# A two-layer hybrid block on one core: pooling groups moved to the front, the last expert's order changed, and expert outputs written by index into one zeroed table

## The chip, the core and the metric

The kernel runs on one core of a Trainium2 chip. The metric is the device time of one execution in microseconds; three executions gave a median of 1464.87 us. The engines are TensorE (PE in the profile; PEld is its weight load), VectorE (DVE), ScalarE (ACT), GpSimd (POOL) and SyncE (SP), which here only issues DMAs. The clock that a profile shows for TensorE is the granted one, as a share of its full speed: 1.00 is 2.4 GHz and 0.50 is 1.2 GHz.

## The reference

Two layers work on 256 tokens of width 1024 and, in layer 0, on 256 context tokens as well (512 tokens in layer 0, 256 in layer 1). A layer is a token mixer of four branches (a Fourier mix, a pooling mix, global attention, window attention), each gated by the normalized input, and a mixture of 16 experts in four groups of four. Cut to what matters here:

```
h   = modulate(rms_norm(x, norm1), sh1, sc1)
# branches: a Fourier, b global attention, c window attention, d pooling
pool: for window w of (2, 4, 8, 16), one per group g of 128 columns:
        pooled[g] = moving_mean(p_in[g], w) - p_in[g]
      out_d[g] = (pooled[g] @ pool_w[g]) * pool_scale[g]
merged = sum_i sigmoid(h @ w_gate[i] + b_gate[i]) * (branch_i @ w_branch[i])
x  = x + g1 * (merged @ w_out)
h2  = modulate(rms_norm(x, norm2), sh2, sc2)
# two experts of one group per token, weights w_top
moe(h2) = sum_e combine[:, e] * ((silu(h2 @ w1[e]) * (h2 @ w3[e])) @ w2[e])
x  = x + g2 * moe(h2)
```

The output is a final RMSNorm of x. All arithmetic is float32.

## The kernel before

Every float32 product is made of three float16 matmuls: each operand is split into a high and a low half, and `mm3` (L577 to L582) adds hi x hi, hi x lo and lo x hi in PSUM. The weights come as float32 by SyncE's DMAs (L219) into tiles called stage, ext or X; ScalarE writes the high half (`whi`, L319), VectorE the low half (`wlo`, L323), and TensorE uses both. So each chunk of weights passes SyncE's queue, ScalarE and VectorE before TensorE has it. All DMAs of SyncE go through one queue in program order. The order within an engine is the order in which a scheduler laid out the program; instructions marked with `keep_in_program_order` stay where the code has them.

**The token mixer.** Global attention runs first, then window attention, each over units of one head pair and one block of queries. A unit's scores S are matmuls of L792 to L796; VectorE takes the row maxima (mx, nm), ScalarE the exponentials E (L811), and both write P in two halves (L824, L825). SyncE transposes P by DMA (into `pair` in layer 0 and `pt` in layer 1), and `values` (L840, output po) multiplies it with V. Between the steps of two units the code calls `next(fill)`: fill is a generator that hands out pieces of other work so that TensorE has something to do while the softmax runs. In window attention it is

```
fill = with_side(chain(spread(gated(1), pool_front(), SPREAD[l]), pool_back(), gated(3)), EV[l][1])
```

`gated(i)` makes branch i's gates (matmuls of hH and hL with a w_gate chunk, a tanh on ScalarE called gate) and multiplies them with the branch matmuls (w_branch). `pool_group(g)` makes the input of pooling group g on TensorE, copies it to SBUF (pool and poolp, L941 and L942), forms the moving sum by shifted additions on VectorE (L944, L947; L955 ends them), and splits the result into pmH and pmL. `mix(g)` multiplies these with the pooling matrix (pwH, pwL) and writes a quarter of branch d (ScalarE L975, VectorE L976). `spread` interleaves the steps of its two generators. Before the change `pool_front` makes groups 0 to 2, and `pool_back` does mix 0, group 3 interleaved with mixes 1 and 2, and mix 3. pmH and pmL have three buffers.

**The experts.** The router gives each token a slot in its two experts; an expert has 96 slots (CAP). `dispatch` gathers a group's tokens by matmuls with one-hot matrices. `up` makes the two hidden products (w1, w3), `hidden` joins them (sa: ScalarE L1388, VectorE L1389; hd is its split), and `down(e)` multiplies by w2 in two halves of 512 columns (py). For experts 0 to 13 ScalarE copies each half to a tile ys (L1333) and issues its DMA into the DRAM tensor `ydram`, 96 rows of 2 KB (L1334). Experts 14 and 15 stay on the chip as yHL and are added by matmuls. `index` computes for each token the two rows of ydram it needs (idx; rows of late experts become row 0 with weight 0). `fetch` (a copy `late` of idx on VectorE, L1445) issues the gathers on GpSimd's queue (L1405: one indirect DMA of 128 rows of 4 KB for each choice and block of 128 tokens), and `combine` weights and adds them (ScalarE L1412, VectorE L1413; in layer 1 also L1415 and L1416, which multiply by the gate g2 and add to x). Each layer has a ydram of its own. In layer 1, `fetch` runs in expert 14's step; in expert 15's step `combine(0)` stands after `up(15, "w1")` and `combine(1)` after `down(14)`. After the 16 experts a branch leads to further rounds for experts with more than 96 tokens; it is not taken with these inputs.

## Time and profile before

| What | Value |
|---|---|
| median of 3 executions | 1464.87 us (1464.43 to 1466.42) |
| the profiled execution's own time | 1468.68 us |
| its span in the trace | 1466.9 us |
| mean granted clock of TensorE | 0.978 |
| TensorE / VectorE / ScalarE / GpSimd busy | 1352.5 / 1119.0 / 953.2 / 14.0 us |
| DMA packets and bytes | 146416, 383.31 MB |
| window attention of layer 0, by the trace | about 240 to 374 us |
| experts of layer 0 | about 575 to 860 us |
| window attention of layer 1 | about 1000 to 1085 us |
| experts of layer 1 | about 1184 to 1445 us |

The trace is one execution; its times count from the span's start. A busy time is the sum of an engine's instructions in a stretch. A wait names the engine and line that waited and what ended the wait. A group of instructions is all those of one line, engine and operation. Matmuls are pipelined, so the length of one is longer than the step from one to the next. For a DMA, the time to landing counts from its issue. A tile's or line's row gives durations as minimum / median / maximum in ns.

### The profile page before, as it was taken

How to read it: one execution, taken by the hardware profiler on the slowest of the kernel's cores; microseconds unless marked ns; L12 is line 12 of the kernel's file. 1: busy time of each engine (PE TensorE's matmuls, PEld its weight loads, DVE VectorE, ACT ScalarE, POOL GpSimd, SP SyncE). 2: the span in 40 equal slices, each digit the busy share in tenths (PEclk: the TensorE clock that was granted, in tenths of full speed). 3: DMA queues.
4: the chain of work that ended last, by engine and by line, in shares of the span. 5: the costliest groups of instructions: out<-in, count | busy, mean ns of one | idle time of the engine just before them, and what ended most of it. 6: DMA issues, size and time to landing. Idle time of an engine off the chain costs nothing. (4 is left out here: it accounts for less than half of the span.)

```text
span 1466.9 us, 33640 instructions
## 1 busy us (share of the span) xinstructions
PE 1352.5 (92%) x14151; PEld 927.0 (63%) x14151; DVE 1119.0 (76%) x2003; ACT 953.2 (65%) x1431; POOL 14.0 (1%) x16
## 2 busy tenths in 40 slices
PE   5999999998999998999999978899989989999984
PEld 3545454444444585777777747587768767777762
DVE  3887647877354557888988888868957888989986
ACT  3777535655233337889898655856845579899971
POOL 0000000000000000000000110000000000000010
PEclk9999999999899999999999999999999999999997
DMA  9559762797685337799999564774979779999981
GB/s 365 207 131 226 228 207 87 198 232 202 187 340 191 120 111 259 270 337 419 397 420 380 222 248 177 188 234 116 232 240 361 263 280 341 418 419 419 399 327 52
DMA packets 146416, 383.31 MB, mean 261 GB/s; under 512 B 91856, under 2 KB 93904, under 8 KB 108112
## 3 DMA queue, kind: packets, MB, share of 16 engines
q1 hardware_dynamic: 133136, 355.24, 68.8%
q10 hardware_dynamic: 11392, 19.56, 3.6%
q0 software_dynamic: 1728, 6.29, 1.2%
q8 instruction: 112, 1.84, 0.5%
q14 instruction: 48, 0.39, 0.1%
HBM read 344.88 MB, written 15.20 MB: 245 GB/s over the span
## 5 line engine op out<-in xcount | busy, mean ns | idle before, releaser
L580 PE MATMUL mm<-hH,whi 128*128 128x96 f16 (+2 forms) x1824 | 398.5, 261 | 3.3 <-ACT whi L319 2.6
L582 PE MATMUL mm<-hH,wlo 128*128 128x96 f16 (+2 forms) x1824 | 398.1, 261 | 1.0 <-DVE wlo L323 0.9
L323 DVE SCALAR_TENSOR_TENSOR wlo<-stage,whi 128x1024 f16<-128x1024 f32 (+1 forms) x212 | 318.9, 1522 | 105.0 <-ACT whi L319 104.3
L581 PE MATMUL mm<-hL,whi 128*128 128x96 f16 (+2 forms) x1824 | 398.2, 261 | 0.0
L580 PEld LDWEIGHTS <-whi 128*128 128x128 f16 x3104 | 304.9, 98 | 75.2 <-issue 4.4
L319 ACT ACTIVATE whi<-stage 128x1024 f16<-128x1024 f32 (+1 forms) x212 | 269.8, 1294 | 126.2 <-PE mm L581 87.1
L582 PEld LDWEIGHTS <-wlo 128*128 128x128 f16 x3104 | 305.0, 98 | 73.7 <-DVE wlo L323 2.7
L581 PEld LDWEIGHTS <-whi 128*128 128x128 f16 x3104 | 305.0, 98 | 72.2 <-issue 2.1
L323 DVE SCALAR_TENSOR_TENSOR wlo<-ext,whi 128x2048 f16<-128x2048 f32 x116 | 262.1, 2287 | 43.2 <-ACT whi L319 43.2
L319 ACT ACTIVATE whi<-ext 128x2048 f16<-128x2048 f32 x116 | 217.8, 1904 | 9.9 <-PE mm L582 7.4
L582 PE MATMUL mm<-xg,wlo 128*128 128x96 f16 x1024 | 132.3, 206 | 0.0
L580 PE MATMUL mm<-xg,whi 128*128 128x96 f16 x1024 | 132.3, 206 | 0.0
L581 PE MATMUL mm<-xg,whi 128*128 128x96 f16 x1024 | 132.3, 206 | 0.0
L581 PE MATMUL py<-wlo,hd 128*96 128x512 f16 x240 | 90.9, 379 | 8.9 <-DVE wlo L323 8.7
L582 PE MATMUL py<-whi,hd 128*96 128x512 f16 x240 | 90.2, 381 | 6.8 <-DVE hd L321 6.0
L580 PE MATMUL py<-whi,hd 128*96 128x512 f16 x240 | 91.0, 379 | 0.0
L580 PE MATMUL mm<-brH,whi 128*128 128x512 f16 (+1 forms) x256 | 83.5, 326 | 0.0
L582 PE MATMUL mm<-brH,wlo 128*128 128x512 f16 (+1 forms) x256 | 83.4, 326 | 0.0
L581 PE MATMUL mm<-brL,whi 128*128 128x512 f16 (+1 forms) x256 | 83.4, 326 | 0.0
L1270 PE MATMUL mm<-Dg,merged 128*128 128x384 f16 x384 | 70.3, 336 | 3.8 <-DVE Dg L1203 1.8
L500 PE MATMUL mm<-stage,cpad 128*32 128x256 f32 x768 | 58.5, 408 | 13.7 <-DMA stage<-in_w_ada_dram 13.6
L825 DVE SCALAR_TENSOR_TENSOR P<-E,rl,P 128x512 f16<-128x512 f32 (+1 forms) x96 | 59.2, 659 | 8.4 <-ACT P L824 8.2
(313 smaller groups left out, 2054.2 us busy)
## 6 DMA issues: line engine op xcount, KB each, us to landing
ext<-in_w_dram SPq DMA_DIRECT2D x118, 1024.0 KB, 9.3
stage<-in_w_dram SPq DMA_DIRECT2D x62, 1024.0 KB, 9.1
stage<-in_w_ada_dram SPq DMA_DIRECT2D x48, 1024.0 KB, 6.0
stage<-in_w_gate_dram SPq DMA_DIRECT2D x32, 1024.0 KB, 5.8
stage<-in_w_in_dram SPq DMA_DIRECT2D x16, 1024.0 KB, 6.7
stage<-in_w_branch_dram SPq DMA_DIRECT2D x32, 512.0 KB, 4.1
ydram<-ys ACTq DMA_DIRECT2D x56, 192.0 KB, 6.9
stage<-in_w_out_dram SPq DMA_DIRECT2D x8, 1024.0 KB, 6.1
```

The lines of the kernel that those rows point to most:

```text
L319: a = nc.scalar.activation(hi, src, AF.Copy, scale=scale)
L323: b = nc.vector.scalar_tensor_tensor(lo, src, scale, hi, op0=ALU.mult, op1=ALU.subtract)
L500: pe.matmul(ps[32 * j:32 * j + 32, :], self.cpad[:, 2 * k:2 * k + 32], st[:, k, :], start=k < 4, stop=k >= 4, tile_position=(0, 32 * j))
L580: pe.matmul(ps, wH(k), xH(k), start=first and k == 0, stop=False)
L581: pe.matmul(ps, wH(k), xL(k), start=False, stop=False)
L582: pe.matmul(ps, wL(k), xH(k), start=False, stop=last and k == nk - 1)
L825: dve.scalar_tensor_tensor(pv[:, 1, qt, :], E[qt][:, 0:nk], r[:, qt:qt + 1], pv[:, 0, qt, :], op0=ALU.mult, op1=ALU.subtract)
L1270: pe.matmul(ps[:, 0:SLOTS], h2[n][t][:, cs(k)], Dg[:, t].rearrange("p e c -> p (e c)"), start=t == 0, stop=t == ntt - 1)
```

## The change

It has five parts.

- **Pooling.** `pool_front` makes all four groups, so group 3 is interleaved with gated(1) as well; `pool_back` is the four mixes alone. pmH and pmL have four buffers.
- **One table, zeroed.** ydram is made once, for both layers. `clear_rows` writes zeros to a seventh of it: a memset of a 128x512 tile on VectorE and one DMA of SyncE (3 x 128 rows of 2 KB, 786 KB). It is called in each unit of layer 0's window attention until the table is done, seven times.
- **Indirect writes.** The two halves of an early expert's output go to ydram by an indirect DMA on GpSimd's queue instead of ScalarE's DMA. Each of the 96 slots has a row number in `rows`; those of empty slots lie outside the table, and the DMA skips them.
- **`filled`.** Six small VectorE operations per layer make `rows` from the counts of the experts, after expert 0's `hidden`. The counts become a lasting tile, and a column of constants is added.
- **End of layer 1.** `combine(0)` moves from behind `up(15, "w1")` to behind `down(14)`, and `combine(1)` from there to behind `hidden(15)`.

```
-LASTING = ("posm", "cw", "cb", "nri", "sp", "se", "ch16")
+LASTING = ("posm", "cw", "cb", "nri", "sp", "se", "ch16", "cnt")
...
+        self.ydram = self.dram.tile([(NE - LATE) * CAP, D], F32, "ydram")
+        self.unset = list(range(0, 21, 3))
...
+    def clear_rows(self):
+        if self.unset:
+            a = self.unset.pop()
+            z = self.wk.tile([128, 512], F32, "zero", tag="t2")
+            self.nc.vector.memset(z, 0.0)
+            rows = self.ydram.rearrange("s (h c) -> (s h) c", h=2).rearrange("(a p) c -> p a c", p=128)
+            self.nc.sync.dma_start(rows[:, a:a + 3, :], z.unsqueeze(1).to_broadcast([128, 3, 512]))
...
-                  {"pmH": 3, "pmL": 3, "a2": 3, "P": 3, "pt": 2 - full, "E": 3, "G": 2})
+                  {"pmH": 4, "pmL": 4, "a2": 3, "P": 3, "pt": 2 - full, "E": 3, "G": 2})
...
+                if full and not glob:
+                    self.clear_rows()
                 next(fill, None)
...
         def pool_front():
             pool_weights()
-            for g in range(3):
+            for g in range(4):
                 yield from pool_group(g)
...
-            mix(0)
-            yield
-            last = pool_group(3)
-            for g in range(1, 3):
-                next(last, None)
+            for g in range(4):
                 mix(g)
                 yield
-            yield from last
-            mix(3)
             pooled["done"] = True
...
-        ydram = self.dram.tile([early * CAP, D], F32, "ydram")
+        ydram = self.ydram
...
-                        act.dma_start(ydram[e * CAP:(e + 1) * CAP, hs], ys)
+                        if not self.dry:
+                            yh = ydram.rearrange("s (h c) -> (s h) c", h=2)
+                            gp.indirect_dma_start(out=yh, in_=ys, in_offset=None,
+                                                  out_offset=bass.IndirectOffsetOnAxis(ap=rows[0:CAP, half, e:e + 1], axis=0),
+                                                  bounds_check=2 * early * CAP - 1, oob_is_err=False)
...
+            def filled():
+                rf = sm.tile([128, 16], F32, "rowf")
+                TT(rf, C("part").to_broadcast([128, 16]), cnt, op=ALU.is_ge)
+                dve.tensor_tensor(rf[0:1, 0:1], rf[0:1, 0:1], rf[0:1, 0:1], op=ALU.subtract)
+                dve.scalar_tensor_tensor(rf, rf, BIG, C("part").to_broadcast([128, 16]), op0=ALU.mult, op1=ALU.add)
+                dve.scalar_tensor_tensor(rf, C("slot", 0, 16), float(CAP), rf, op0=ALU.mult, op1=ALU.add)
+                for half in range(2):
+                    dve.tensor_scalar(rows[:, half, :], rf, 2.0, float(half), op0=ALU.mult, op1=ALU.add)
...
                 pa = up(e, "w1")
-                if e == NE - 1 and pe_all:
-                    combine(0, True)
...
                     down(e - 1, prev)
                 if e == NE - 1 and pe_all:
-                    combine(1, True)
+                    combine(0, True)
...
                 prev = hidden(e, pa, pb)
+                if e == NE - 1 and pe_all:
+                    combine(1, True)
+                if e == 0:
+                    filled()
```

How this moves instructions shows at three places. In the rows, `x2` is two such instructions in a row, and the line numbers of the changed kernel are its own (L319 becomes L320, L323 L324, L811 L823, L824 L836, L1013 L1021, L975 L989, L1413 L1425).

ScalarE at the end of layer 0's window attention, before; L824 is P, L811 E, L319 with po the split of the attention output, L941, L942 and pmH a pooling group, L975 a mix:

```order
L941 ACTIVATE pool_4356<-mm 128x256
L942 ACTIVATE poolp<-mm 128x256
L811 ACTIVATE E,ls<-S,nm 128x256 x2
L816 ACTIVATE es<-nm,sink 128x2
L824 ACTIVATE P<-E,rl 128x256 x2
L319 ACTIVATE brH_2938<-po 128x256
L811 ACTIVATE E,ls<-S,nm 128x256 x2
L816 ACTIVATE es<-nm,sink 128x2
L444 DMA sink<-in_sink_dram 128x8
L319 ACTIVATE pmH<-poolp 128x256
L824 ACTIVATE P<-E,rl 128x256 x2
L975 ACTIVATE brH_4189<-mm,psl 128x512
```

And in the changed kernel, the last units of the same attention:

```order
L320 ACTIVATE whi<-stage 128x1024
L836 ACTIVATE P<-E,rl 128x256 x2
L823 ACTIVATE E,ls<-S,nm 128x256 x2
L828 ACTIVATE es<-nm,sink 128x2
L320 ACTIVATE whi<-stage 128x1024
L836 ACTIVATE P<-E,rl 128x256 x2
L1021 ACTIVATE gate<-mm,hbg 128x512
L320 ACTIVATE adah<-mm 128x256
L823 ACTIVATE E,ls<-S,nm 128x256 x2
L828 ACTIVATE es<-nm,sink 128x2
L456 DMA sink<-in_sink_dram 128x8
L836 ACTIVATE P<-E,rl 128x256 x2
```

The pooling copies and both pmH are gone from among the last units; the last mix now stands ahead of these rows, and a gate and weight splits stand between the units.

ScalarE at the end of layer 1's window attention, before; gate is the tanh of gated(3):

```order
L319 ACTIVATE whi<-stage 128x1024
L975 ACTIVATE brH_19113<-mm,psl 128x256
L824 ACTIVATE P<-E,rl 128x512 x2
L319 ACTIVATE whi<-stage 128x1024
L941 ACTIVATE pool_19154<-mm 128x256
L942 ACTIVATE poolp<-mm 128x256
L975 ACTIVATE brH_19113<-mm,psl 128x256 x2
L319 ACTIVATE whi<-stage 128x1024
L319 ACTIVATE brH_18273<-po 128x256
L319 ACTIVATE pmH<-poolp 128x256
L975 ACTIVATE brH_19113<-mm,psl 128x256
L1013 ACTIVATE gate<-mm,hbg 128x256
```

And in the changed kernel:

```order
L989 ACTIVATE brH_19313<-mm,psl 128x256 x3
L320 ACTIVATE whi<-stage 128x1024
L836 ACTIVATE P<-E,rl 128x512 x2
L320 ACTIVATE brH_18424<-po 128x256
L989 ACTIVATE brH_19313<-mm,psl 128x256
L320 ACTIVATE whi<-stage 128x1024
L1021 ACTIVATE gate<-mm,hbg 128x256
L320 ACTIVATE whi<-stage 128x1024
L1021 ACTIVATE gate<-mm,hbg 128x256
L320 ACTIVATE brH_18424<-po 128x256
```

The last split of po now comes after two gates, where it came before the last mix and the first gate; no pooling copy is left.

VectorE in the last expert of layer 1, before; L1296 and L1297 are slot weights, yHL with py the output split of expert 14, wlo from X the last weight split, L1413, L1415 and L1416 the combination:

```order
L1445 COPY late<-idx 128x4
L1296 TENSOR_SCALAR slotw_25133<-mm 96x2
L1297 TENSOR_TENSOR slotw<-slotw_25133 96x1
L323 SCALAR_TENSOR_TENSOR wlo<-ext,whi 128x2048 x2
L1413 SCALAR_TENSOR_TENSOR yg<-yg,wr 128x1024
L323 SCALAR_TENSOR_TENSOR yHL<-py,slotw,yHL 96x512
L1415 TENSOR_TENSOR yg<-yg,merged 128x1024
L323 SCALAR_TENSOR_TENSOR wlo<-X_24636,whi 128x2048
L1416 TENSOR_TENSOR X_4729<-X_4729,yg 128x1024
L323 SCALAR_TENSOR_TENSOR yHL<-py,slotw,yHL 96x512
L1413 SCALAR_TENSOR_TENSOR yg<-yg,wr 128x1024
L1389 SCALAR_TENSOR_TENSOR sa<-mm,sa 128x384
```

And in the changed kernel, where these three lines are L1425, L1427 and L1428:

```order
L1457 COPY late<-idx 128x4
L1304 TENSOR_SCALAR slotw_25344<-mm 96x2
L324 SCALAR_TENSOR_TENSOR wlo<-ext,whi 128x2048
L1305 TENSOR_TENSOR slotw<-slotw_25344 96x1
L324 SCALAR_TENSOR_TENSOR wlo<-X_24847,whi 128x2048
L324 SCALAR_TENSOR_TENSOR yHL<-py,slotw,yHL 96x512 x2
L1425 SCALAR_TENSOR_TENSOR yg<-yg,wr 128x1024
L1427 TENSOR_TENSOR yg<-yg,merged 128x1024
L1425 SCALAR_TENSOR_TENSOR yg<-yg,wr 128x1024
L1428 TENSOR_TENSOR X_4751<-X_4751,yg 128x1024
L1401 SCALAR_TENSOR_TENSOR sa<-mm,sa 128x384
```

The last weight split and both output splits moved ahead of the first step of the combination; sa of expert 15 stands behind four steps of the combination, as before, but all four now come right ahead of it.

On GpSimd's queue, 28 writes a layer now stand ahead of the gathers, and each waits for the landing of the one before it. On SyncE's queue the seven DMAs of zeros stand among the loads and transposes of layer 0's window attention.

## Rows read from the trace of the kernel before

**Rows 1.** The page: busy time, share of the span and instructions of each engine.

```profile
PE 1352.5 (92%) x14151; PEld 927.0 (63%) x14151; DVE 1119.0 (76%) x2003; ACT 953.2 (65%) x1431; POOL 14.0 (1%) x16
```

**Rows 2.** Stretches: us; busy PE, PEld, DVE, ACT, POOL; clock; DMA share, GB/s.

```profile
245.00:300.00 55.00, 54.32 (x321) 25.11 (x320) 45.17 (x124) 35.44 (x77) 0.00 (x0) 1.00 0.67 191
300.00:354.00 54.00, 53.53 (x385) 26.63 (x383) 39.33 (x102) 30.63 (x77) 0.00 (x0) 1.00 0.87 217
364.00:375.00 11.00, 7.70 (x29) 3.14 (x28) 7.96 (x25) 4.58 (x13) 0.00 (x0) 0.52 0.71 183
660.00:820.00 160.00, 155.45 (x2297) 123.41 (x2295) 142.63 (x84) 140.16 (x134) 0.00 (x0) 1.00 1.00 405
1020.00:1060.00 40.00, 38.37 (x350) 31.24 (x349) 39.89 (x95) 33.80 (x67) 0.00 (x0) 1.00 0.90 229
1072.50:1078.00 5.50, 5.50 (x33) 3.90 (x33) 0.48 (x1) 0.47 (x1) 0.00 (x0) 0.53 0.46 177
```

**Rows 3.** TensorE's waits, 354 to 375: us in total, times, longest.

```profile
PE S L792 <- ACT E L811: 5.1, 1, 5.1
PE mm L580 <- ACT pmH L319: 2.7, 1, 2.7
```

**Rows 4.** ScalarE's timeline, 354 to 372: start, length, what, idle before.

```profile
359.40 1.06 ACT L319 ACTIVATE whi<-stage 128x1024 f16<-128x1024 f32 x1 [2.71 <-DMA stage<-in_w_gate_dram]
```

**Rows 5.** Groups of VectorE's instructions by line.

```profile
L947 DVE TENSOR_TENSOR pool<-pool 128x269 f32<-128x269 f32 (+2 forms) x18 | 7.7, 428 | 0.0
...
L1421 DVE SCALAR_TENSOR_TENSOR inr<-sp,inr 128x8 f32<-128x8 f32 (+1 forms) x2 | 0.3, 154 | 0.0
```

**Rows 6.** ScalarE's waits, 245 to 354.

```profile
ACT whi L319 <- DMA stage<-in_w_gate_dram: 4.0, 1, 4.0
```

**Rows 7.** TensorE's waits, 1060 to 1080.

```profile
PE po L840 <- DMA pt<-P: 6.5, 1, 6.5
```

**Rows 8.** Instructions that write or read ydram: ns, first and last start.

```profile
L1334 ACTq DMA_DIRECT2D ydram<-ys x56: 310/311/342, 604.7 to 1413.0; - x56
L1405 POOL DMA_INDIRECT yg<-ydram,late x12: 933/937/2442, 838.8 to 1428.1; - x12
...
DMA to landing us min/median/max: 2.9/6.8/8.6
```

**Rows 9.** Waits of ScalarE, TensorE and SyncE's queue, 1200 to 1425.

```profile
ACT ys L1333 <- PE py L582: 13.9, 17, 3.0
...
PE py L582 <- DVE hd L321: 4.8, 4, 1.5
PE py L581 <- DVE wlo L323: 4.5, 4, 1.6
...
SPq L219 <- DMA ydram<-ys: 53.4, 10, 10.7
```

**Rows 10.** ScalarE's ys in 1325 to 1425, and sa in 600 to 840.

```profile
L1333 ACT ACTIVATE ys<-py x12: 574/586/594, 1330.9 to 1412.4; 96x512 f32<-96x512 f32 x12
...
L1388 ACT ACTIVATE sa<-mm x15: 474/476/480, 609.0 to 835.9; 128x384 f32<-128x384 f32 x15
```

**Rows 11.** GpSimd's timeline, 1415 to 1432.

```profile
1421.95 2.44 POOL L1405 DMA_INDIRECT yg<-ydram,late  x1 [573.41 <-DMA stage<-in_w_dram]
```

**Rows 12.** ScalarE's timeline, 1420 to 1446.

```profile
1427.83 1.15 ACT L1412 ACTIVATE yg<-yg,wr 128x1024 f32<-128x1024 f32 x1 [3.66 <-DMA yg<-ydram,late]
```

**Rows 13.** VectorE's timeline, 1415 to 1443.

```profile
1421.29 4.50 DVE L323 SCALAR_TENSOR_TENSOR wlo<-ext,whi 128x2048 f16<-128x2048 f32 x2
1432.52 1.29 DVE L1413 SCALAR_TENSOR_TENSOR yg<-yg,wr 128x1024 f32<-128x1024 f32 x1 [6.74 <-DMA yg<-ydram,late]
...
1441.75 0.56 DVE L1389 SCALAR_TENSOR_TENSOR sa<-mm,sa 128x384 f32<-128x384 f32 x1 [0.97 <-PE mm L582]
```

**Rows 14.** TensorE's waits, 1416 to 1445.

```profile
PE acc L1339 <- DVE yHL L323: 3.2, 1, 3.2
```

**Rows 15.** The page: one of the costliest groups, busy us and mean ns.

```profile
L323 DVE SCALAR_TENSOR_TENSOR wlo<-ext,whi 128x2048 f16<-128x2048 f32 x116 | 262.1, 2287 | 43.2 <-ACT whi L319 43.2
```

More of the change, by code (lines that the diff above doesn't have):

```diff
@@ L49 @@
     ("ident", 128), ("blk2", 2), ("sel2", 2),
-    ("slot", CAP), ("rank0", 4), ("invc", 64),
+    ("slot", CAP), ("rank0", 4), ("invc", 64), ("part", 1),
 )
@@ L83, in shape_constants @@
     c["slot"] = np.tile(np.arange(CAP), (128, 1))
+    c["part"] = p[:, None].astype(np.float64)
     c["rank0"] = np.tile(3 - np.arange(4), (128, 1))
@@ L1447, in fetch @@
                     gather(t, late)
+            rows = sm.tile([128, 2, 16], U32, "rows")
+            def filled():
[6 more added lines that the diff above has]
+                    dve.tensor_scalar(rows[:, half, :], rf, 2.0, float(half), op0=ALU.mult, op1=ALU.add)
             run_all(dispatch(0))
@@ L1522, in moe @@
                 dve.tensor_scalar(sp_, sp_, -float(CAP), None, op0=ALU.add)
+                dve.tensor_scalar(cnt, cnt, -float(CAP), None, op0=ALU.add)
                 W = Stream(self, 10 + l, 1, "ext")
```

## The prediction

> **What bounds the kernel now.** I read the page's busy times first, then the table of stretches, then the waits and timelines of the stretches that the change touches. TensorE is busy for 92% of the span, VectorE for 76%, ScalarE for 65%, GpSimd for 1% [rows 1]. So an edit is worth what it takes out of TensorE's idle time and the low clock behind that, and a cost counts only where it ends up as TensorE waiting. In the table of stretches [rows 2] the reader is to see where that can be: TensorE is full in most of layer 0's window attention (54.32 of 55 us, 53.53 of 54) and nearly so in the expert stage (155.45 of 160), where the DMA engines are full as well (share 1.00, 405 GB/s). It is not full at the end of layer 0's window attention (7.70 of 11 us, clock 0.52), and the waits below name two more places, the same end in layer 1 and the last expert of layer 1. The change touches all three, and both expert stages.
>
> **Pooling, layer 0: -8 us.** In 354 to 375 TensorE waits 5.1 us for the exponentials E and 2.7 us for pmH, the split of the last pooling group [rows 3]. ScalarE stood 2.71 us of this for a w_gate load [rows 4], with a weight split, the pooling copies and pmH queued behind that load and ahead of E (the order of ScalarE's rows above shows them). In the new order no pooling copy is left among the last scores, and mixes and gate matmuls, which wait for neither, stand between them. Behind the idle time the clock is at about the half level, 0.52 over 364 to 375, where TensorE was busy for 7.70 us [rows 2]; at the full level that work takes half, so 3.9 us more can come back. The most is 5.1 + 2.7 + 3.9 = 11.7. The 2.71 us of the late load stay, since no part of the change fetches it earlier, and some clock loss stays with them: I take 8, with ends 0 and 11.7. What is late next there is that w_gate load.
>
> **Zeroing the table: +2 us.** Seven memsets of 128x512 and seven SyncE DMAs of 786 KB go into the first seven units of this attention. The nearest row of VectorE, an addition of 128x269, takes 0.43 us [rows 5]; by columns a memset is 0.8 at most, some 6 us together, under a TensorE that is full there [rows 2]; if that cover is gone, it is 6 us. The DMAs carry 5.5 MB, at 405 GB/s [rows 2] 13.6 us of transfers. From 245 to 354 the DMA engines are idle for 33% of 55 and 13% of 54 us, 25 us together [rows 2], so they fit on the whole. But ScalarE already waits 4.0 us for one load there [rows 6], and on SyncE's queue the zeroing stands ahead of loads and of the transposes of P. Ends 0 and 13.6; 2, since that wait of ScalarE's left TensorE full.
>
> **Pooling, layer 1: -5 us.** TensorE stands 6.5 us for the transposed P of the last pair [rows 7]. Its next 5.5 us are at clock 0.53 [rows 2]: at most 6.5 + 2.7 = 9.2. The new order puts 48 gate, 8 branch and 3 pooling matmuls of 256 columns between the last scores and those values. In 1020 to 1060 TensorE does one in 40 / 350 = 0.114 us [rows 2], so this is 59 x 0.114 = 6.7 us of work that needs no P, just the length of the wait. Against it, a pooling group's VectorE work moves up into that stretch, where VectorE is busy 39.89 of 40 us [rows 2]: some six operations of 0.43 us [rows 5] and a few small ones, 3 us. Hence 5; ends 0 and 9.2.
>
> **The writes: 0.** ScalarE issues 56 DMAs less, 0.31 us each [rows 8]. None of its waits in the expert stage of layer 1 is on a DMA, its largest sum being 13.9 us for py, and TensorE's are on hd and wlo from VectorE [rows 9]; so 17.4 us of ScalarE's queue buy nothing I can point to. SyncE waited 53.4 us on semaphores that these writes hold [rows 9], yet as the weights arrive before ScalarE wants them, loads sent sooner only wait longer. The same goes for the bytes. Running the reference's router on its inputs fills 858 of 1344 slots in layer 0 and 473 in layer 1, so 486 and 871 rows of 4 KB, 5.6 MB, are not written: 14 us of transfers at 405 GB/s that nobody waits for. The Trainium skill (SBUF — State Buffer, "A bandwidth-pool intuition that's wrong") says that HBM is almost always the end-to-end bottleneck; the share of 1.00 agrees, the waits do not, and by that sentence the 14 us would be gained as well.
>
> The new cost is a chain. On GpSimd's queue every write waits for the one before it to land, since all write one table. No row shows an indirect write. Its nearest rows are the gather, 0.94 us on GpSimd, 2.44 at the longest, and the old write, landing 2.9 to 8.6 us after issue, median 6.8 [rows 8]. By these a link takes between 0.94 + 2.9 = 3.8 and 2.44 + 8.6 = 11.0 us. An expert has two. From the first ys at 1330.9 to the twelfth at 1412.4, the halves of one expert being some 2.3 us apart, an expert takes (81.5 - 2.3) / 5 = 15.8 us in layer 1, and in layer 0 (835.9 - 609.0) / 14 = 16.2 [rows 10]. The chain costs nothing while a link stays below 7.9. I take 6.5, from the gather: the first of layer 1, 512 KB, began at 1421.95 and was used at 1427.83, 5.9 us with 2.44 of GpSimd's [rows 11, 12], and a write carries 4 to 8 times less, though among more traffic. So the chain costs nothing by itself, except at the end.
>
> **Slot indices: +1 us.** Six small VectorE operations a layer, 0.15 us each as their kind has [rows 5], come after expert 0's hidden layer: 0.9 us a layer on an engine 89% busy in 660 to 820 [rows 2]. Ends 0 and 2.
>
> **End order, layer 1: -2 us.** Before, VectorE stood 6.74 us for the gathers [rows 13] with an output split (yHL) and the last weight split behind it, and TensorE waited 3.2 us for yHL [rows 14]. In the new order both splits stand ahead of the combination. But the gathers now wait for the last link: by the same 2.3 us the chain of the last expert begins 2.3 ahead of the last half at 1412.4 [rows 10], and two links of 6.5 end 13 later, near 1423, 1 us behind the first gather's old start at 1421.95 [rows 11]; and sa of the last expert, at 1441.75 [rows 13], still stands behind VectorE's first steps of the combination. 3.2 less 1: 2; ends -4, with some clock, and +2.
>
> **Sum.** -8 + 2 - 5 + 0 + 1 - 2 = -12. The profiled execution took 1468.68 us (span 1466.9), 3.81 above the median of 1464.87; taken from that median, **1453 us**. All good ends together are -11.7 - 9.2 - 4 = -25, so 1440. A difference under 0.2%, 2.9 us, is one that a measurement of this kernel can't tell from none.
>
> **Rivals.**
> (a) The chain sets the pace (slower). Place: GpSimd's queue through both expert stages; it decides from 7.9 us a link. With the old write's median, 0.94 to 2.44 + 6.8, a link is 7.7 to 9.2. At 8.6 layer 1 falls behind by 17.2 - 15.8 = 1.4 us an expert over 13 experts, less some 6 us, my estimate of how long a stored half can wait until its buffer is wanted: +12; layer 0 likewise +7: 1453 + 19 = 1472. For it: those medians, full DMA engines. Against: GpSimd's gather was away in less, and empty slots shorten the write.
> (b) GpSimd holds VectorE up. The gather that ran beside two wlo took 2.44 us against 0.94 [rows 8, 11], so GpSimd does wait; the two wlo took 4.50 us [rows 13], 2.25 each, where the mean is 2.287 [rows 15], so VectorE does not. Were each of 28 writes to hold VectorE for 0.94, that is 26 us a layer, against some 27 us of idle VectorE in 250 (11%, as in 660 to 820 [rows 2]); if half of that can be used, +13 a layer: 1479. The Trainium skill (SBUF — State Buffer, the "DVE blocks DMA" trap) has a GpSimd-issued DMA starved of descriptors while VectorE is in a two-port mode, and advises the ACT or SP queue; by it links would grow, as in (a), and the gather's 2.44 agrees.
> (c) The DMA engines bound the expert stages, and the unwritten rows pay: 1453 - 14 = 1439. Against: the waits [rows 9].
> (d) The waits at the three places only change their names, as when the late w_gate load or the zeroing holds the same end: -1 or -2, some 1464.
>
> **How the numbers follow.** Forecast 0.64, (a) 0.16, (b) 0.05, (c) 0.05, (d) 0.10. The forecast's own range is 1441 to 1462. Reaching to (d) and to part of (a) the range is 1441 to 1470, with about 0.05 left out below and 0.13 above. Faster by over 0.2%: forecast and (c) with a little of (d), 0.71; within 0.2%: most of (d) and the mild part of (a), 0.10; slower: 0.19.
>
> **What would show it.** Right: in the new profile TensorE's waits on E, on pmH and on pt at the two attention ends are gone or under 2 us and the clock there stays at 1.0; the step between sa activations stays near 16 us; the first gather of layer 1 begins within 2 us of where the last ys had put it, 9.5 us behind it. A link longer than 7.9 us, with ScalarE waiting for an ys buffer in the middle of an expert stage, proves (a); wlo longer than 2.3 us beside a write proves (b); a pace under 15 us proves (c). Waits for weight or P loads of over 5 us more in 245 to 354 would prove the zeroing mis-sized. The forecast is wrong if either attention end keeps its idle time.

## The result

The changed kernel takes 1487.65 us, median of 4 runs (1487.45 to 1487.93), against 1465.52 for the kernel before (1464.43 to 1466.42): a ratio of 1.0151, 95% interval 1.0134 to 1.0169. It is 22 us slower, where 12 us faster were forecast and 1470 was the top of the range. The profiled execution has a span of 1486.0 us, 19.1 above that of before.

The page of the changed kernel, busy time and the two DMA queues that changed most (packets, MB, share):

```profile
PE 1355.0 (91%) x14151; PEld 926.6 (62%) x14151; DVE 1124.0 (76%) x2022; ACT 958.2 (64%) x1431; POOL 104.4 (7%) x72
...
q0 software_dynamic: 5312, 11.76, 2.3%
q10 hardware_dynamic: 5120, 8.54, 1.6%
```

Against [rows 1], TensorE is busy for as long (1355.0 against 1352.5 us), VectorE and ScalarE within 5 us; GpSimd went from 14.0 to 104.4 us. So no engine that computes got more work to speak of. All queues together moved as much as before (383.29 MB against 383.31): ScalarE's lost 11.0 MB (19.56 before), GpSimd's gained 5.5 (6.29 before), and SyncE's gained the 5.5 MB of zeros. The time is in waits.

The table of stretches of the changed kernel, the two attention ends and the experts of layer 1 (columns as in [rows 2]):

```profile
345.00:375.00 30.00, 28.83 (x214) 14.14 (x213) 23.00 (x71) 19.02 (x51) 0.00 (x0) 0.97 0.80 244
1055.00:1085.00 30.00, 28.73 (x277) 23.17 (x278) 29.49 (x67) 22.93 (x50) 0.00 (x0) 1.00 0.84 229
1200.00:1425.00 225.00, 205.00 (x3104) 163.86 (x3101) 194.03 (x109) 194.66 (x185) 42.01 (x25) 0.98 0.93 366
```

And TensorE's waits there, first in 340 to 385, then in 1060 to 1100:

```profile
PE S L804 <- ACT E L823: 3.9, 2, 2.7
...
PE S L804 <- ACT E L823: 0.8, 2, 0.4
```

Both ends did what was forecast. In layer 0 TensorE now waits 3.9 us, where it waited 5.1 + 2.7 [rows 3], and the clock is 0.97 in 345 to 375, where the kernel before has 0.77 (0.52 in 364 to 375 [rows 2]). In layer 1 the wait of 6.5 us for pt [rows 7] is gone and the clock stays at 1.00. What came instead is in the expert stages. The starts of sa, first and last, in layer 0 without its first expert and in layer 1 with all sixteen, for the changed kernel:

```profile
L1400 ACT ACTIVATE sa<-mm x15: 472/475/477, 601.4 to 837.5; 128x384 f32<-128x384 f32 x15
...
L1400 ACT ACTIVATE sa<-mm x16: 472/475/483, 1202.8 to 1445.3; 128x384 f32<-128x384 f32 x16
```

and for the kernel before in layer 1:

```profile
L1388 ACT ACTIVATE sa<-mm x16: 472/476/483, 1196.9 to 1420.9; 128x384 f32<-128x384 f32 x16
```

In layer 0 fourteen steps take 837.5 - 601.4 = 236.1 us, where they took 226.9 [rows 10]. In layer 1 fifteen steps take 242.5 us, where they took 224.0: 18.5 us more. Steps outside a dispatch were 14.8 or 14.9 and 13.3 us in turn before; now each is 15.1. Of those with a dispatch in layer 1, the longest went from 17.6 to 19.9. Another 11 us lie between the last sa of layer 0 and the first of layer 1 (365.3 us, against 354.2 in the third run below, which has the same pooling; two executions of one kernel, the fourth run and its repetition, differ by 5 us there, 351.5 and 356.7). Who waits is in the waits of TensorE and VectorE, layer 1, changed kernel:

```profile
PE py L594 <- DVE hd L322: 13.3, 11, 1.5
PE mm L1278 <- ACT hH L1280: 5.1, 4, 1.8
...
DVE wlo L324 <- ACT whi L320: 29.1, 30, 3.7
```

and of VectorE in the same stage before:

```profile
DVE wlo L323 <- ACT whi L319: 15.9, 16, 2.2
```

TensorE waits 13.3 us for hd, the split of the hidden layer, 11 times; before it was 4.8 us and 4 times [rows 9]. VectorE waits for ScalarE's weight splits 29.1 us instead of 15.9. None of these waits is for a write. (The 5.1 us for hH belong to the dispatch.) ScalarE's hd, in turn, now waits for VectorE's part of sa more often; in the same stretches, the changed kernel and before:

```profile
ACT hd L320 <- DVE sa L1401: 11.6, 11, 1.1
...
ACT hd L319 <- DVE sa L1389: 4.1, 5, 1.1
```

The order of ScalarE's instructions in one expert of layer 1 shows what differs. Before:

```
L1388 ACTIVATE sa<-mm 128x384
L319 ACTIVATE whi<-ext 128x2048
L319 ACTIVATE hd_22165<-sa 128x384
L319 ACTIVATE whi<-ext 128x2048 x2
L319 ACTIVATE whi<-X_21785 128x2048
L1333 ACTIVATE ys<-py 96x512
L319 ACTIVATE whi<-stage 128x2048
L1334 DMA ydram<-ys 96x512
L1333 ACTIVATE ys<-py 96x512
L319 ACTIVATE whi<-stage 128x2048
L1334 DMA ydram<-ys 96x512
```

Changed:

```
L1400 ACTIVATE sa<-mm 128x384
L320 ACTIVATE whi<-ext 128x2048 x2
L320 ACTIVATE hd_22340<-sa 128x384
L320 ACTIVATE whi<-ext 128x2048
L320 ACTIVATE whi<-X_21956 128x2048
L1341 ACTIVATE ys<-py 96x512
L320 ACTIVATE whi<-stage 128x2048
L1341 ACTIVATE ys<-py 96x512
L320 ACTIVATE whi<-stage 128x2048
```

With the two DMA issues gone from ScalarE, the scheduler put hd behind two weight splits of 1.9 us in every expert; before, it stood behind one in the fifth, ninth and thirteenth expert of each layer, in the fifteenth of layer 0, and in layer 1 also in the three in which a dispatch begins. (The front part shows moved instructions at three places; the expert stages are a fourth.) VectorE's order moved with it: outside the dispatches its part of sa starts 4.5 us behind ScalarE's, one weight split later than before, when it was 2.3 in most experts. From the start of ScalarE's sa to that of VectorE's hd, on which TensorE waits, it took 5.0 us before in the experts with steps of 13.3, where hd stood behind one split, and 7.2 or more where it stood behind two; now it takes 7.2 or more in every expert. That this costs the time is a suspicion until the runs below separate it from the chain. The chain is there as well. GpSimd's timeline of the changed kernel (start, length, what, idle before and what ended it):

```profile
1267.77 0.92 POOL L1344 DMA_INDIRECT ydram<-ys,rows  x1 [6.62 <-DMA ydram<-ys,rows]
1276.32 2.59 POOL L1344 DMA_INDIRECT ydram<-ys,rows  x1 [7.63 <-DMA ydram<-ys,rows]
...
1402.75 0.92 POOL L1344 DMA_INDIRECT ydram<-ys,rows  x1 [6.76 <-DMA ydram<-ys,rows]
1411.28 2.47 POOL L1344 DMA_INDIRECT ydram<-ys,rows  x1 [7.61 <-DMA ydram<-ys,rows]
1420.30 1.09 POOL L1344 DMA_INDIRECT ydram<-ys,rows  x1 [6.55 <-DMA ydram<-ys,rows]
1427.74 1.11 POOL L1344 DMA_INDIRECT ydram<-ys,rows  x1 [6.35 <-DMA ydram<-ys,rows]
1432.41 1.32 POOL L1344 DMA_INDIRECT ydram<-ys,rows  x1 [3.56 <-DMA ydram<-ys,rows]
1436.04 3.03 POOL L1344 DMA_INDIRECT ydram<-ys,rows  x1 [2.32 <-ACT whi L320]
1444.47 2.32 POOL L1417 DMA_INDIRECT yg<-ydram,late  x1 [5.40 <-DVE slotw L1304]
```

From 1402.75 to 1427.74 three links take 8.33 us each, above the 7.9 at which a pair is as long as an expert; the links of layer 1 that waited for no ys range from 6.3 to 10.2 before the loads run out. The gather behind the last write, at 1444.47, came when VectorE had made `late`, the copy of the indices, at 1443.54, just ahead of the slotw that the profile names; the chain did not hold it. And the tile ydram, changed kernel (ns min/median/max, first and last start):

```profile
L1344 POOL DMA_INDIRECT ydram<-ys,rows x56: 917/1467/3036, 597.4 to 1436.0; - x56
...
DMA to landing us min/median/max: 2.9/5.6/8.1
```

A write lands 5.6 us after its issue in the middle, 8.1 at most, and the next waits for that landing.

### The profile page after: what moved, and what is told of

Read it like the earlier page. It is cut to its first block, busy times and chain, and to the rows that moved or that the text cites. A ratio compares the mean times of both kernels' runs of the same rounds, so it can differ in the third digit from the quotient of the medians.

```text
span 1486.0 us, 33761 instructions
## 1 busy us (share of the span) xinstructions
PE 1355.0 (91%) x14151; PEld 926.6 (62%) x14151; DVE 1124.0 (76%) x2022; ACT 958.2 (64%) x1431; POOL 104.4 (7%) x72
## 2 busy tenths in 40 slices
DMA packets 146530, 383.29 MB, mean 258 GB/s; under 512 B 93314, under 2 KB 95362, under 8 KB 108224
## 5 line engine op out<-in xcount | busy, mean ns | idle before, releaser
L324 DVE SCALAR_TENSOR_TENSOR wlo<-stage,whi 128x1024 f16<-128x1024 f32 (+1 forms) x212 | 319.1, 1521 | 112.9 <-ACT whi L320 112.3
L320 ACT ACTIVATE whi<-stage 128x1024 f16<-128x1024 f32 (+1 forms) x212 | 269.6, 1294 | 126.3 <-PE mm L593 85.7
L324 DVE SCALAR_TENSOR_TENSOR wlo<-ext,whi 128x2048 f16<-128x2048 f32 x116 | 262.6, 2287 | 58.4 <-ACT whi L320 55.4
L320 ACT ACTIVATE whi<-ext 128x2048 f16<-128x2048 f32 x116 | 217.6, 1900 | 15.1 <-issue 7.6
L1344 POOL DMA_INDIRECT ydram<-ys,rows x56 | 90.5, 1616 | 1328.5 <-ACT ys L1341 1078.7
```

Source lines behind the costliest of these rows:

```text
L320: a = nc.scalar.activation(hi, src, AF.Copy, scale=scale)
L324: b = nc.vector.scalar_tensor_tensor(lo, src, scale, hi, op0=ALU.mult, op1=ALU.subtract)
L1344: gp.indirect_dma_start(out=yh, in_=ys, in_offset=None, out_offset=bass.IndirectOffsetOnAxis(ap=rows[0:CAP, half, e:e + 1], axis=0), bound ...
```

## The experiments

Three theories for the expert stages: **O**, the new order on ScalarE; **C**, the chain of writes; **Q**, GpSimd's queue as such, by its descriptors beside VectorE. The first four runs were on one chip with the kernel before at 1466.8 us, the next four with it at 1465.94, the last four with it at 1465.3.

**Unchained writes on GpSimd** (e1_gpsimd_direct).

```
-                            gp.indirect_dma_start(out=yh, in_=ys, in_offset=None,
-                                                  out_offset=bass.IndirectOffsetOnAxis(ap=rows[0:CAP, half, e:e + 1], axis=0),
-                                                  bounds_check=2 * early * CAP - 1, oob_is_err=False)
+                        gp.dma_start(ydram[e * CAP:(e + 1) * CAP, hs], ys)
...
-                if e == 0:
-                    filled()
```

> The changed kernel, but each half of an early expert goes to its own 96 rows of the table by a plain DMA on GpSimd's queue: all slots are written, no write waits for the one before it, no row numbers are computed. The order of instructions on ScalarE stays that of the changed kernel (hd of every expert behind two weight splits). Theory O (the order: without ScalarE's DMA issues the scheduler puts hd behind two splits where it stood behind one in every third expert or so): no gain, 1483 to 1490 us, steps between sa activations of 15.1 us. Theory C (the chain of writes paces the experts): the chain is gone, so some 30 us come back, about 1457 us, steps of 13.3 and 14.8. Theory Q (GpSimd's queue as such, its descriptors beside VectorE): about 1487 too, but with longer wlo (over 2.35 us) in the trace.

Measured: 1483.52 us, ratio 1.0111 (1.008 to 1.0141), and steps of 15.1. GpSimd waits for nothing but ys, and TensorE still for hd (waits of GpSimd and of TensorE in 1240 to 1400):

```profile
POOL ydram L1342 <- ACT ys L1341: 157.5, 19, 17.6
...
PE py L594 <- DVE hd L322: 8.5, 7, 1.5
```

The starts of sa, both layers:

```profile
L1396 ACT ACTIVATE sa<-mm x15: 474/474/477, 603.2 to 839.2; 128x384 f32<-128x384 f32 x15
...
L1396 ACT ACTIVATE sa<-mm x16: 471/474/481, 1200.0 to 1442.5; 128x384 f32<-128x384 f32 x16
```

236.0 and 242.5 us, where the changed kernel has 236.1 and 242.5: in that kernel the chain adds nothing to the experts' steps. The chain is gone and the time is not, so C alone does not explain it. O and Q stand. The 4 us that this run is faster lie between the layers (360.8 us from sa to sa, against 365.3). There the changed kernel has one wait behind the last expert of layer 0 that this run lacks, in 835 to 1000; what held VectorE's sa there the profile does not name:

```profile
PE py L1326 <- DVE sa L1401: 4.1, 1, 4.1
```

**A small issue back on ScalarE** (e2_small_issue_on_scalare): the indirect writes as changed, and

```
+                        act.dma_start(self.spare_rows[e:e + 1, hs], ys[0:1, :])
```

> The changed kernel with its indirect writes and their chain, and beside each of them a 2 KB DMA on ScalarE's queue that copies one row of ys to a spare DRAM tensor nobody reads. With this issue on ScalarE the scheduler lays out ScalarE as in the kernel before (hd behind one split in every expert where it stood so). Theory O: the steps of 13.3 us come back, 1457 us, up to 1466 if the chain then becomes the limit, because two links of 8 us are longer than 15 us. Theory C: unchanged or a little slower, 1486 to 1491. Theory Q: unchanged, 1486 to 1491.

Measured: 1468.54 us over 10 runs (1462.2 to 1472.67), ratio 1.0005 (0.9985 to 1.0024). A 2 KB DMA beside each write makes the kernel 19 us faster, since it brings back the old order, on ScalarE and on VectorE; the step of 13.3 us returns where nothing else holds it. But something else holds some. ScalarE's waits in 590 to 840 and in 1200 to 1425 now have a line that the changed kernel's did not:

```profile
ACT sa L1402 <- DMA ydram<-ys,rows: 7.3, 3, 3.7
...
ACT sa L1402 <- DMA ydram<-ys,rows: 5.9, 6, 1.8
```

sa needs a buffer that a write has not yet left: the chain, which the slower order had hidden.

**Direct writes on ScalarE** (e3_direct_on_scalare): the changed kernel with the old line `act.dma_start(ydram[e * CAP:(e + 1) * CAP, hs], ys)` and without `filled`.

> The changed kernel with ScalarE's direct writes of the kernel before (into the one zeroed table), no row numbers; pooling, zeroing and end order stay changed. All three theories: the expert stages run as before, steps of 13.3 and 14.8 us; what is left are pooling, zeroing and the end order. By the first place of the new trace (8 us ahead at the start of the experts of layer 0) and the two later ones: about 1453 to 1458 us. If it stays near 1487, none of them holds and the expert stages are slowed by the other parts.

Measured: 1452.49 us, ratio 0.9911 (0.9882 to 0.994). The starts of sa, both layers:

```profile
L1396 ACT ACTIVATE sa<-mm x15: 473/476/481, 600.9 to 827.8; 128x384 f32<-128x384 f32 x15
...
L1396 ACT ACTIVATE sa<-mm x16: 472/476/486, 1182.0 to 1406.0; 128x384 f32<-128x384 f32 x16
```

226.9 and 224.0 us, the same as before the change. With the writes undone, what is left of the change is worth 14 us, and the expert stages are untouched by it.

**Without zeroing** (e4_direct_no_zeroing, and once more on another chip as e12_direct_no_zeroing_again): as the third run without

```
-                if full and not glob:
-                    self.clear_rows()
```

> As the run before, without the zeroing of the table (its memsets and DMAs are left out; every row that is read is written anyway). The difference from it is the price of the zeroing: the trace of the changed kernel fell back by 5 us at its window attention's third unit and by 5 more near the eighth, and had made up most of it at the end of that attention. Zeroing hidden: the same time within 2 us. Zeroing on the path: 4 to 10 us faster, about 1447 to 1452 us.

Measured: 1448.35 us, ratio 0.9882 (0.9859 to 0.9905), 4.1 under the third run beside it, but the two intervals overlap. The traces show the place. The row of 310 to 345, of this run:

```profile
310.00:345.00 35.00, 35.00 (x250) 17.36 (x248) 24.31 (x66) 19.42 (x49) 0.00 (x0) 1.00 0.84 248
```

and of the changed kernel:

```profile
310.00:345.00 35.00, 32.24 (x233) 15.95 (x232) 23.08 (x61) 18.07 (x44) 0.00 (x0) 0.98 0.83 234
```

ScalarE's wait for the gate weights in 310 to 350, of this run:

```profile
ACT whi L320 <- DMA stage<-in_w_gate_dram: 5.2, 2, 2.9
```

and of the changed kernel:

```profile
ACT whi L320 <- DMA stage<-in_w_gate_dram: 8.5, 2, 6.1
```

TensorE loses 2.8 us there with the zeroing, and ScalarE waits 3.3 us more. The third run, which differs from this one by the zeroing alone, has the same: TensorE 32.08 us, and 9.0 us of ScalarE's wait. The second time:

> The fourth run again, on the same chip as the run before, as what it is compared with: 1446 to 1451 us.

Measured: 1451.85 us, ratio 0.9907 (0.9879 to 0.9934). The same kernel differs by 3.5 us between the two sets, so single differences of that size between sets are not read here.

**Unchained writes on GpSimd with the small issue** (e5_gpsimd_direct_and_small_issue): the first run's and the second run's edit together.

> Plain, unchained writes on GpSimd's queue as in the first run, and beside each the 2 KB DMA on ScalarE's queue of the second, which gives ScalarE the order of the kernel before. Theory O with the chain as a second, separate limit: both limits are gone, so the time is that of the direct writes on ScalarE, 1452 to 1458 us, steps of 13.3 and 14.8. Theory Q (GpSimd's queue as such is slow, whatever the order): 1468 to 1484. If it stays near the 1468.5 of the second run, the small issues cost the 16 us that are left there, and not the chain.

Measured: 1454.19 us, ratio 0.9922 (0.9897 to 0.9948), steps of 13.3 and 14.8. TensorE's waits in 1240 to 1400:

```profile
PE py L594 <- DVE wlo L324: 4.5, 4, 1.6
PE py L595 <- DVE hd L322: 3.0, 2, 1.5
```

This is the run that decides. From the first run it differs by the small issue on ScalarE alone, and is 29 us faster: that is the order, and Q falls, since all writes still go through GpSimd's queue. The order is that of all engines: in the expert stages of this run ScalarE, VectorE and TensorE have the sequences of the kernel before. Which of the moved instructions costs how much is argued from the waits above; no run moves hd alone. From the second it differs by plain writes in place of chained indirect ones, without row numbers, and is 14 us faster.

**Two tables** (e9_two_tables): the second run with one table for each half of the columns, so that a write waits for the last but one.

```
+        self.ydram = [self.dram.tile([(NE - LATE) * CAP, 512], F32, f"ydram{h}") for h in range(2)]
...
+                            gp.indirect_dma_start(out=ydram[half], in_=ys, in_offset=None,
+                                                  out_offset=bass.IndirectOffsetOnAxis(ap=rows[0:CAP, half, e:e + 1], axis=0),
+                                                  bounds_check=early * CAP - 1, oob_is_err=False)
...
+                        for h in range(2):
+                            gp.indirect_dma_start(out=yg[:, h * 512:h * 512 + 512], out_offset=None, in_=ydram[h],
+                                                  in_offset=bass.IndirectOffsetOnAxis(ap=idx[:, r, t:t + 1], axis=0))
```

> The second run (indirect writes, small issue on ScalarE, order of the kernel before) with two tables, one for each half of the columns, each zeroed. Each write waits for the one but last instead of the last, so an expert's pair of links takes one landing, some 8 us, instead of two; the gathers become twice as many. Theory C as the second limit (the chain costs the 16 us that the second run keeps over the direct writes): 1453 to 1460 us, some of it for the longer row of gathers; no wait of ScalarE's sa on a write. If indirect writes cost by themselves (GpSimd's time of 0.9 to 3.0 us, or what they do to VectorE): 1466 to 1470, as the second run.

Measured: 1463.59 us, ratio 0.9985 (0.9969 to 1.0001). The time lies between the two expectations, but the trace tells them apart. The starts of sa:

```profile
L1402 ACT ACTIVATE sa<-mm x15: 472/476/484, 597.9 to 826.5; 128x384 f32<-128x384 f32 x15
...
L1402 ACT ACTIVATE sa<-mm x16: 473/476/486, 1190.6 to 1414.0; 128x384 f32<-128x384 f32 x16
```

228.6 and 223.4 us: layer 1 runs as with direct writes, layer 0 with 1.7 more in its last step but one, and no sa waits for a write. So indirect writes cost the expert stages next to nothing once two of them may be under way; the chain was the second limit. What this version still lost against direct writes lies elsewhere in its trace: between the last sa of layer 0 and the first of layer 1 (364.1 us against 354.2), where sixteen gathers stand instead of eight, and in the tail. That the gathers are the cause of all of it was not tried apart.

**The parts of the good half.** e6_no_end_change is the fourth run with `combine(0)` and `combine(1)` back in their old places:

> Direct writes on ScalarE, no zeroing, and the end order of layer 1 as before the change; only the pooling order is changed. Against the fourth run (1448.35) the difference is what the end order gives: by the prediction 2 us with writes that land later, with direct writes up to 4, so 1449 to 1453 us. If the end order gives nothing: 1448.

Measured: 1452.99 us, ratio 0.991 (0.9877 to 0.9942). e7_no_pooling_change is the fourth run with `pool_front`, `pool_back` and the buffers of before:

> Direct writes on ScalarE, no zeroing, pooling as before the change; only the end order of layer 1 is changed. If the two attention ends give what the traces show with the zeroing taken out (about 8 to 10 us in layer 0 and 7 in layer 1), this is 1463 to 1465 us, 2 us under the kernel before. If most of the gain had come from elsewhere, it is nearer to 1450.

Measured: 1465.32 us, ratio 0.9998 (0.9984 to 1.0012). So the end order alone is worth nothing that this can tell, and the pooling alone 13 us (1465.94 before, beside both), both attention ends together. By the traces of these two, one execution each, layer 0's first sa comes 5.1 us earlier with the new pooling (587.6 against 592.7), and from layer 0's last sa to layer 1's first it is 6.8 us less (353.8 against 360.6).

**Half of the bytes** (e10_half_the_bytes): the third run with `act.dma_start(ydram[e * CAP:e * CAP + CAP // 2, hs], ys[0:CAP // 2, :])`.

> The third run (direct writes on ScalarE, zeroed table) where each write carries only its first 48 rows; slots 48 to 95 stay zero in the table, so that part of the experts' output is left out. Half of 11.0 MB less is written, as much as empty slots save. If bytes in the expert stages pay (rival c of the prediction): 1452 less 13, about 1440 us, steps under 13.3. If they don't: 1450 to 1454, the same steps of 13.3 and 14.8.

Measured: 1765.3 us, which says nothing: with half of the experts' output left out in layer 0 the routing of layer 1 changed, and its branch to further rounds was taken (48 sa in the trace instead of 32). The stages before that branch are still to be read. The starts of sa in layer 0 and in layer 1's first round:

```profile
L1396 ACT ACTIVATE sa<-mm x15: 471/476/482, 603.5 to 830.4; 128x384 f32<-128x384 f32 x15
...
L1396 ACT ACTIVATE sa<-mm x16: 471/475/486, 1186.3 to 1411.9; 128x384 f32<-128x384 f32 x16
```

226.9 us in layer 0, to the tenth what they were: with half the bytes written no step got shorter. (In layer 1 the inputs of the experts differ; 225.6.) The bytes do not pay there.

**hd still earlier, twice.** e8_hd_first puts the split of the fourth run's hd under the scheduler's high priority:

> The fourth run with the split of the hidden layer (hd) put at a higher priority for the scheduler: in the three experts of each layer that follow a dispatch's first half, hd stands right behind sa instead of behind the copies of the dispatch. Theory O says that TensorE's wait for hd sets the pace where hd comes late; if it was late in these experts too, up to 1.5 us for each of six, 1440 to 1447 us; if the copies set the pace there, 1448.

Measured: 1453.02 us, ratio 0.992 (0.9892 to 0.9949), the same as the run without the end change beside it: nothing gained. The trace shows that it tried little: hd moved ahead of the dispatch's copies, not ahead of a weight split. e11_two_issues_per_half cuts each direct write of the fourth run in two DMAs:

> The fourth run (direct writes on ScalarE, no zeroing) with each write cut in two of 48 rows, so 56 issues more on ScalarE. The scheduler then puts hd behind one weight split in every expert instead of every third or so. Theory O: the steps of 14.8 us become 13.3, in some four or five experts of each layer, 8 to 15 us in all: 1434 to 1441. If the place of hd is not what sets the step: 1448, or up to 1452 for the added issues.

Measured: 1447.76 us, ratio 0.9885 (0.9864 to 0.9906), although hd now stood behind one split nearly everywhere. Its twin of the same set, the second execution of the fourth run, took 1451.85, but the two intervals overlap. The starts of sa:

```profile
L1395 ACT ACTIVATE sa<-mm x15: 474/475/482, 599.1 to 822.1; 128x384 f32<-128x384 f32 x15
...
L1395 ACT ACTIVATE sa<-mm x16: 471/476/544, 1178.0 to 1410.0; 128x384 f32<-128x384 f32 x16
```

Layer 0's fourteen steps took 223.0 us in place of 226.9; layer 1's did not get shorter (232.0 us, of which the last step, in which the order differs, took 14.6 in place of 7.8). Outside the dispatches the steps became nearly even: 13.3 to 14.1 in layer 0 and 14.1 to 14.5 in layer 1, in place of 13.3 and 14.8 or 14.9 in turn. The row for two such experts of layer 1:

```profile
1367.00:1395.20 28.20, 27.25 (x433) 22.09 (x430) 28.20 (x17) 25.23 (x21) 0.00 (x0) 1.00 0.99 384
```

VectorE is busy for all of the 28.2 us. So theory O, carried on, was wrong about the next gain, 8 to 15 us: an expert without dispatch costs VectorE 14.1 us. The old order was already near that on average (13.3 and 14.8), the changed one was 1.0 us above it, and a better place of hd finds at most the 4 us of layer 0.

## Why the prediction was wrong

**Pooling: right in sum.** -8 and -5 were forecast for the two ends, 13 together; the run with that part alone is 13 us under the kernel before (1452.99 against 1465.94). That the sum fits so well is in part luck: by the traces the ends gave about 5 and 7. Of TensorE's remaining 3.9 us, 2.7 (at 342.77) stand behind a w_gate load for which ScalarE waits 6.1 us; these are the zeroing's, since the run without it has no such wait. At the end itself 1.2 are left (365.94), just behind 1.1 us of ScalarE's wait for a w_gate load, which is what was named as late next.

**Zeroing: right in sign and about in size**, +2 forecast, some 4 found (with overlapping intervals), of which the trace shows 2.8 where it happens; the mechanism named, ScalarE's waits for loads, is the one in the rows.

**End order and slot indices: too small to check one by one.** -2 and +1 were forecast; the kernel with the end order alone is at 0.9998 of before, within 2 us.

**The step that failed is "The writes: 0".** It argued that taking 56 issues of 0.31 us off ScalarE buys nothing, because ScalarE's issue is not what anyone waits for. As time that was right: 56 issues more, in the last of the runs above, cost nothing either. But a scheduler lays out the engines' programs, and without these issues it put hd one weight split later in the experts where it had stood early, and VectorE's sa with it. The sum has no term for that: the orders of the expert stages differed, and the prediction prices only the issues and the chain there. Yet [rows 9] named hd as what TensorE waited for most there: a swap in the producer of the longest wait is a term of the sum. The whole change of order measures +29 us (first against fifth run).

**The link was mis-sized: 6.5 forecast, 8.3 found.** The estimate came from the gather's start, in a stretch with little other traffic (DMA share 0.47 in 1421 to 1428 of the kernel before, 0.95 in 1400 to 1421); the old write's median of 6.8 with GpSimd's 0.94 to 2.44 on top, which rival (a) used, was the better row. With 8.3 rival (a) is true in kind, and worth 14 us once the order is mended (second against fifth run). In the changed kernel itself the two overlap: order and chain together cost 1487.65 - 1454.19 = 33 us, where 29 and 14 would make 43 if they added up. Taken out alone (first run), the chain gives back 4, none of it in the experts' steps. So its zero there came true by luck: not because a link was under 7.9 us, but because the late hd had made the steps longer.

**The other rivals.** (b) falls: two runs send 56 writes through GpSimd and leave the expert stages as with direct writes, and VectorE's long wlo take 2287 ns in the mean in the changed kernel too. The changed kernel's writes hold GpSimd for 917 ns at the least, 1467 in the middle and 3036 at most; the plain writes of the first run, from the same queue and beside the same splits, 512 ns and 702 at most. So whatever stretches GpSimd's part here stretches the indirect writes and hardly the plain ones. The rule of the Trainium skill (SBUF — State Buffer, the "DVE blocks DMA" trap), by which a GpSimd-issued DMA is starved of descriptors while VectorE runs in a two-port mode, is not borne out by these plain writes; whether the splits run in such a mode no row shows. Its advice to keep to the ACT or SP queue was the better one here, for another reason than its own. (c) falls: half the bytes, the same steps in layer 0. The sentence of the Trainium skill quoted for it (SBUF — State Buffer, "A bandwidth-pool intuition that's wrong") does not hold for these stages: their DMA engines are full, but ScalarE waits for no load there [rows 9]. (d) shows only in the 2.7 us of the zeroing's load.

In sum, against before: pooling -13, end order and indices about 0, zeroing +4, the writes +33, which makes +24; measured +22, and the parts come from sets of runs that differ by up to 3.5.

The version that beats both kernels is the fourth run: pooling and end order as changed, direct writes on ScalarE, no zeroing. It took 1448.35 and 1451.85 us, ratios 0.9882 and 0.9907.

## What to carry over

Before an instruction that "costs nothing" is taken off an engine, compare the two built orders around every instruction that someone waits for; where the scheduler decides, the removal can cost more than the instruction ever did. Count a chain of dependent DMAs by the landing time under the traffic of that very stage, and compare a round of the chain with a round of the loop. And when one limit is lifted, look for the one just under it: here the late hd hid the chain, and behind both stood VectorE's 14.1 us an expert.

## What was unexpected of the hardware

In these traces the length of a link hardly depends on what it carries. By the router on the inputs, expert 3 of layer 1 has all 96 slots filled and expert 12 has 6. The write that began at 1267.77 is the first half of expert 3 and was followed 8.55 us later; the one at 1420.30 is the first half of expert 12, followed 7.44 us later. The longest of layer 1 that waited for no ys, 10.24 us (from 1361.42), is the second half of expert 8, with 22 filled slots. No run chains writes of full experts only, but by these links skipping empty slots shortened the chain by little, while the DMA engines were busy with weights (share 0.93 in 1200 to 1425, first fence of stretches above). At the end, when the loads have run out, the last links take 4.67 and 3.61 us (1427.74, 1432.41, 1436.04).
